# Gate and up projections of three feed-forwards as seven block products of 2x2 blocks

## Chip, cores and metric

The kernel runs on one core of a Trainium2 chip. The metric is device time in microseconds, the median over runs. Only the order and number of operations on the chip count; the host lays arrays out beforehand.

## Reference, cut to what matters

Two transformer blocks run one after the other on 512 tokens of width 1024, in float32. Between them they have five feed-forwards (numbered 0 to 4 here), all of inner width F = 2816. In a feed-forward every token row is normalised, projected twice (gate and up), combined and projected down:

```python
def swiglu_ffn(h, w_gate_up, w_down):
    g, u = jnp.split(h @ w_gate_up, 2, axis=-1)
    return (jax.nn.silu(g) * u) @ w_down

h = h + HALF_STEP * swiglu_ffn_2(rms_norm_2(h, ffn1_norm[layer]),
                               ffn1_w_gate[layer], ffn1_w_up[layer], ffn1_w_down[layer])
```

The second block has four of them: feed-forward 1 before a convolution module, 2 behind it, 3 before an attention layer, 4 behind it, the last before the final norm. Everything else (sparse attention, a recurrent mixer, cross attention, convolution, stick-breaking attention) stays as it is.

## The kernel before, in words

Activations lie transposed: x is eight tiles of 128 features by 512 tokens. The product of a weight tile and an activation tile in float32 is made of three matmuls in the shorter type float32r: every operand is split into a high part (ScalarE copies it, L127, or L133 with the norm's gain) and a low part (VectorE subtracts, L131, L134), and `mm3` (L170) adds high x high, high x low and low x high into one PSUM bank. `load_w` (L160) brings 128 output columns of a weight matrix (128 x 1024) in through SP's queue and splits them; there are three raw buffers and four of each split half.

`ffn` (L304) does a feed-forward in two halves of 11 F tiles. For each F tile it loads the gate and the up weights, makes both projections over all 512 tokens (8 K tiles x 3 matmuls each, L200), and `up` (L309) multiplies both with the tokens' inverse norms (row tile `rb`), applies Silu and splits the product into `hh` and `hl`. Then eight down products (L328, 11 F tiles x 3 matmuls) are added to x by the callback in `half_ffn` (L1031). With `head=2` (feed-forwards 0 and 1) the first two F tiles are made in token halves of 256, so that TensorE can start while the second half of the tokens is still being normalised (`post_norm_add`, L279, writes x on GpSimd at L294); with `tail=2` (0 and 4) the last two down products are made in halves.

The order on each engine's queue is set by a list scheduler of the framework, by program order and readiness in its own model of time; between `order_pe` and `free_pe` TensorE's order is the program's. `inv_rms_chain` (L233) places the few matmuls of the norm's sums between others, `tick` by `tick`. PSUM has eight banks under four names, which `mm_tile` and `at_tile` take in turn (`turn`, L65).

```python
for half in range(2):
    ...
    for p in range(FH):
        ...
            pg = mm_tile()
            proj(pg, g, xs)
            pu = at_tile()
            proj(pu, u, xs)
        h.append(up(p, pg, pu))
    ...
    for n in range(KT - nt):
        pd = mm_tile() if n % 2 else at_tile()
        down(half, n, load_down(n), pd, h)
        out_cb(half, n, pd, WHOLE)
```

Feed-forward 1 follows a norm that is finished token half by token half; 2 follows the convolution's output projection, whose callback (L1191) updates x tile by tile; 4 follows the attention's output projection in the same manner (L1351).

Of the kernel before, what the change touches and what calls it, by code (L numbers as in the profile page):

```python
# [25 lines left out]
NSA_H = 8  # L26
BUCKETS = 32
BW = 640
WHOLE = slice(0, S)
HALVES = (slice(0, S // 2), slice(S // 2, S))  # L30

# [17 lines left out]
def kernel(ctx: ExitStack, tc: tile.TileContext, t: dict, out: bass.AP):  # L49
# [24 lines left out]
    def mm_tile():  # L74
        return next_tile("mm")
# [91 lines left out]
        split(raw, hi, lo, pieces=pieces, hp=hp)  # L167
        return hi, lo

    def mm3(ps, lh, ll, rh, rl, start, stop):  # L170
        nc.tensor.matmul(ps, lh, rh, start=start, stop=False)  # L171
        nc.tensor.matmul(ps, lh, rl, start=False, stop=False)  # L172
        nc.tensor.matmul(ps, ll, rh, start=False, stop=stop)  # L173


    chain = []
# [127 lines left out]
    def ffn(fp, xs, st, wg, wu, wd, out_cb, head=0, tail=0, step=None):  # L304


        r = []

        def up(p, pg, pu):  # L309
            if not r:  # L310
                r.append(inv_rms(st)[1])
            rb = r[0]
            gr = fp.tile([P, S], F32, tag="gr", bufs=2, name=nm("gr"))
            nc.vector.tensor_tensor(gr, pg, rb, ALU.mult)
            nc.scalar.activation(gr, gr, AF.Silu)
            su = fp.tile([P, S], F32, tag="su", bufs=2, name=nm("su"))
            nc.vector.tensor_tensor(su, pu, rb, ALU.mult)  # L317
            nc.vector.tensor_tensor(su, su, gr, ALU.mult)
            hh = fp.tile([P, S], F32R, tag=f"hh{p}", name=nm("hh"))
            hl = fp.tile([P, S], F32R, tag=f"hl{p}", name=nm("hl"))  # L320
            split(su, hh, hl)
            return hh, hl

        def down(half, n, ws, pd, h, ts=WHOLE):
            for k in range(FH):
                hi, lo = ws[k // 6]
                sl = slice(k % 6 * P, (k % 6 + 1) * P)
                mm3(pd[:, ts], hi[:, sl], lo[:, sl], h[k][0][:, ts], h[k][1][:, ts], k == 0, k == FH - 1)  # L328
                tick()

        for half in range(2):
            h = []
            nh = 0 if half else head
            ws = [[load_w(w[n], D, pieces=4) for w in (wg, wu)] for n in range(nh)]
            pss = [(mm_tile(), mm_tile()) for n in range(nh)]
            for ts in HALVES:
                for n in range(nh):
                    projs(list(zip(pss[n], ws[n])), xs, ts)
            free_pe()
            if nh:  # L340
                order_pe()
                got = inv_rms_chain(st, 4, 6)
                pss.append(tuple(at_tile() for _ in range(2)))
                for ps, w in zip(pss[nh], (wg, wu)):
                    proj(ps, load_w(w[nh], D), xs)
                free_pe()
                r.append(got[1])
            for p in range(FH):
                n = half * FH + p
                if p < len(pss):  # L350
                    pg, pu = pss[p]
                else:
                    g = load_w(wg[n], D)
                    u = load_w(wu[n], D)
# [6 lines that stand above are left out]
            def load_down(n):  # L361
                return [load_w(wd[half, n][:, a * P : b * P], (b - a) * P) for a, b in ((0, 6), (6, FH))]

            nt = tail if half else 0
# [4 lines that stand above are left out]
            ws = {n: load_down(n) for n in range(KT - nt, KT)}  # L369
            pds = {n: mm_tile() if n % 2 else at_tile() for n in ws}  # L370
            if nt:
                order_pe()
            for ts in HALVES:
                for n in ws:
                    down(half, n, ws[n], pds[n], h, ts)
                    out_cb(half, n, pds[n], ts)
                if nt and step:
                    step(ts)

# [647 lines left out]
    def half_ffn(xs, st, idx, nxt, head=0, tail=0, step=None, ap=False):  # L1027
        st2, xs2 = {}, []

        def cb(half, n, ps, ts):  # L1030
            last_add[0] = nc.vector.scalar_tensor_tensor(x[n][:, ts], ps[:, ts], 0.5, x[n][:, ts], ALU.mult, ALU.add)  # L1031
            if half == 1:
                if nxt is not None:
                    xs2.append(split_x(n, nxt))
                square_acc(x[n], n, st2, ts, ap)

        with tc.tile_pool(name=f"fp{idx}", bufs=1) as fp:
            ffn(fp, xs, st, t[f"wg{idx}"], t[f"wu{idx}"], t[f"wd{idx}"], cb, head, tail,
                step and (lambda ts: step(st2, ts)))
        return xs2, st2  # L1040

    xs, st = half_ffn(xs, st, 1, "mix_norm_0", head=2)


    rt, rb = inv_rms(st)
    cs = ExitStack()
    cp = cs.enter_context(tc.tile_pool(name="cp", bufs=1))
# [466 lines left out]
```

## Time and profile before

| | |
|---|---|
| median of 3 runs | 2797.47 us (2797.16 to 2798.1) |
| the profiled execution's own time | 2799.96 us |
| its span, first to last instruction | 2798.2 us |
| mean granted TensorE clock | 0.994 of full speed |
| feed-forwards 1, 2 and 4 begin in the trace at about | 861, 1424 and 2425 us |

The profile is of one execution. PE is TensorE's matmuls, PEld its weight loads, DVE VectorE, ACT ScalarE, POOL GpSimd, SP the queue that issues most transfers. A matmul's start is recorded, its end is modelled, so rates are read from the distance of starts. A group of instructions shows how many there were, how long they were busy in all and on the mean, and how long the engine had been idle just before them and for whom.

### The profile page before, as it was taken

How to read it: one execution, taken by the hardware profiler on the slowest of the kernel's cores; microseconds unless marked ns; L12 is line 12 of the kernel's file. 1: busy time of each engine (PE TensorE's matmuls, PEld its weight loads, DVE VectorE, ACT ScalarE, POOL GpSimd, SP SyncE). 2: the span in 40 equal slices, each digit the busy share in tenths (PEclk: the TensorE clock that was granted, in tenths of full speed). 3: DMA queues.
4: the chain of work that ended last, by engine and by line, in shares of the span. 5: the costliest groups of instructions: out<-in, count | busy, mean ns of one | idle time of the engine just before them, and what ended most of it. 6: DMA issues, size and time to landing. Idle time of an engine off the chain costs nothing.

```text
span 2798.2 us, 35182 instructions
## 1 busy us (share of the span) xinstructions
PE 2731.0 (98%) x13750; PEld 2252.2 (80%) x13750; DVE 1465.1 (52%) x2270; ACT 1074.5 (38%) x1772; POOL 339.0 (12%) x451
## 2 busy tenths in 40 slices
PE   8999999999999999999899999999999997999998
PEld 6877988888888888885788888898888874788887
DVE  7666564643436434449754344534444489543443
ACT  5676544422334323331333233343223366332223
POOL 0133132200002000012210000100000136200001
PEclk9999999999999999999999999999999999999999
DMA  5312321223222233236332322323232320222322
GB/s 194 105 46 99 114 76 53 93 85 109 98 83 92 91 99 103 82 110 171 83 113 87 102 98 85 111 84 104 82 109 89 107 65 4 83 96 85 107 84 81
DMA packets 86923, 263.19 MB, mean 94 GB/s; under 512 B 9655, under 2 KB 13751, under 8 KB 86756
## 3 DMA queue, kind: packets, MB, share of 16 engines
q1 hardware_dynamic: 85148, 258.42, 29.6%
q10 hardware_dynamic: 1608, 2.52, 0.3%
q8 instruction: 108, 1.77, 0.3%
q14 instruction: 59, 0.48, 0.1%
HBM read 256.60 MB, written 4.30 MB: 93 GB/s over the span
## 4 chain that ended last, share of the span: by engine, by line
PE 79%; DVE 4%; issue 1%; DMA 1%; ACT 1%; POOL 0%; SPq 0%; DVEq 0%; ACTq 0%
PE sc L171 9%; PE sc L172 9%; PE sc L173 9%; PE mm L172 7%; PE mm L173 7%; PE mm L171 7%; PE tr L171 6%; PE tr L172 6%; PE tr L173 6%; PE po L171 3%; PE po L172 3%; PE po L173 3%; DVE wlo L131 1%; PE po L1311 1%; DVE c L1114 1%
## 5 line engine op out<-in xcount | busy, mean ns | idle before, releaser
L127 ACT ACTIVATE whi<-wraw 128x1024 fp32r<-128x1024 f32 (+3 forms) x518 | 492.3, 955 | 1287.4 <-PE sc L172 430.7
L131 DVE TENSOR_TENSOR wlo<-wraw,whi 128x1024 fp32r<-128x1024 f32 (+4 forms) x559 | 581.1, 1049 | 384.4 <-ACT whi L127 383.1
L171 PE MATMUL mm<-xh,whi 128*128 128x512 f32 (+1 forms) x760 | 287.7, 379 | 6.3 <-ACT whi L127 5.9
L172 PE MATMUL mm<-xl,whi 128*128 128x512 f32 (+1 forms) x760 | 286.9, 377 | 5.5 <-DVE xl L134 5.5
L173 PE MATMUL mm<-xh,wlo 128*128 128x512 f32 (+1 forms) x760 | 286.4, 377 | 0.0
L171 PE MATMUL sc<-xh,whi 128*128 128x512 f32 (+1 forms) x696 | 270.1, 388 | 0.0
L172 PE MATMUL sc<-xl,whi 128*128 128x512 f32 (+1 forms) x696 | 269.2, 387 | 0.0
L173 PE MATMUL sc<-xh,wlo 128*128 128x512 f32 (+1 forms) x696 | 269.2, 387 | 0.0
L172 PE MATMUL tr<-xl,whi 128*128 128x512 f32 (+1 forms) x592 | 222.8, 376 | 3.1 <-DVE xl L134 3.1
L171 PE MATMUL tr<-xh,whi 128*128 128x512 f32 (+1 forms) x592 | 223.1, 377 | 0.0
L173 PE MATMUL tr<-xh,wlo 128*128 128x512 f32 (+1 forms) x592 | 222.9, 376 | 0.0
L216 POOL TENSOR_TENSOR sqacc<-sq,sq 128x512 f32<-128x512 f32 (+1 forms) x11 | 16.3, 1486 | 1585.7 <-issue 896.0
L317 DVE TENSOR_TENSOR su<-sc,rb 128x512 f32<-128x512 f32 x80 | 55.3, 691 | 252.6 <-PE sc L173 252.6
L171 PEld LDWEIGHTS mm<-xh,whi 128*128 128x128 f32 x760 | 144.3, 190 | 33.2 <-ACT whi L127 5.9
L172 PEld LDWEIGHTS mm<-xl,whi 128*128 128x128 f32 x760 | 144.2, 190 | 31.9 <-DVE xl L134 7.1
L173 PEld LDWEIGHTS mm<-xh,wlo 128*128 128x128 f32 x760 | 144.2, 190 | 25.1 <-DVE wlo L131 0.3
L171 PEld LDWEIGHTS sc<-xh,whi 128*128 128x128 f32 x696 | 130.7, 188 | 29.6 <-issue 2.5
L173 PEld LDWEIGHTS sc<-xh,wlo 128*128 128x128 f32 x696 | 130.7, 188 | 26.5
L172 PEld LDWEIGHTS sc<-xl,whi 128*128 128x128 f32 x696 | 130.7, 188 | 26.3
L171 PE MATMUL sc<-hh,whi 128*128 128x512 f32 (+1 forms) x352 | 132.6, 377 | 0.0
L172 PE MATMUL sc<-hl,whi 128*128 128x512 f32 (+1 forms) x352 | 132.2, 376 | 0.0
L173 PE MATMUL sc<-hh,wlo 128*128 128x512 f32 (+1 forms) x352 | 132.2, 376 | 0.0
(531 smaller groups left out, 5554.0 us busy)
## 6 DMA issues: line engine op xcount, KB each, us to landing
wraw<-wg SPq DMA_DIRECT2D x110, 512.0 KB, 3.4
wraw<-wu SPq DMA_DIRECT2D x110, 512.0 KB, 3.4
wraw<-wd SPq DMA_DIRECT2D x80, 384.0 KB, 3.0
wraw<-wd SPq DMA_DIRECT2D x80, 320.0 KB, 2.8
wraw<-w_pw SPq DMA_DIRECT2D x24, 512.0 KB, 3.5
wraw<-w_in_f SPq DMA_DIRECT2D x15, 512.0 KB, 4.1
R<-glscr SPq DMA_DIRECT2D x28, 264.0 KB, 5.3
x<-xT SPq DMA_DIRECT2D x16, 256.0 KB, 5.9
```

Of the source, the lines that this page charges most:

```text
L127: last_hi[0] = nc.scalar.activation(hi[:, sl], src[:, sl], AF.Copy)
L131: nc.vector.tensor_tensor(lo[:, sl], src[:, sl], f32(hi[:, sl]), ALU.subtract)
L171: nc.tensor.matmul(ps, lh, rh, start=start, stop=False)
L172: nc.tensor.matmul(ps, lh, rl, start=False, stop=False)
L173: nc.tensor.matmul(ps, ll, rh, start=False, stop=stop)
L216: eng.tensor_tensor(state["acc"][:, ts], state["first"][:, ts], sq[:, ts], ALU.add)
L317: nc.vector.tensor_tensor(su, pu, rb, ALU.mult)
L1114: nc.vector.scalar_tensor_tensor(d, tap(k), v("w_dw", 31 * j + k), d, ALU.mult, ALU.add)
L1311: nc.tensor.matmul(po[64 * hx : 64 * hx + 64, j * P :], vsh[:, j, c0 : c0 + 64], PTs[hx][:, o : o + n_], start=j == 0, stop=j == NT - 1)
```

## The change

Feed-forwards 1, 2 and 4 get a new function, `ffn_blocks`. It takes two F tiles at a time and regards x (two K halves by two token halves) and the weights (two F tiles by two K halves) as 2x2 blocks. Seven products of sums and differences of blocks, instead of eight products of blocks, give the four blocks of the result (the scheme of Strassen in Winograd's form). Each product has gate and up side by side in one bank: 2 lanes x 4 K tiles x 3 matmuls of 256 tokens.

- `block_sums` forms four combinations of the token and K halves of x, once per feed-forward: 256-column operations on VectorE, a subtraction on GpSimd, and splits into high and low parts.
- `weights` loads the four weight blocks of a pair (gate and up side by side, 512 columns each), forms three further combinations with four 128 x 1024 additions on GpSimd, and splits seven operands instead of four.
- `product` accumulates into banks A (products 1, 4, 6, 7), B (2) and E (3, 5). What has to be kept between is copied out by ScalarE or subtracted by VectorE; `block` then does what `up` did, for 256 tokens at a time, with the up multiply on GpSimd for three of four blocks.
- The F tiles go in three chunks (8, 8 and 6 tiles) instead of two halves, each with its eight down products.
- `mm3` gets an argument that leaves out a check of accumulation groups; its three matmuls stay the same. After feed-forward 1 the turn of PSUM banks is set anew.
- The two-halves start of feed-forward 1 is replaced by the first two products of two pairs, which need the first token half alone.

The diff, cut to its core:

```diff
...
+BLOCKED = {1: "ffn1_norm_0", 2: "ffn2_norm_0", 4: "ffn2_norm_1"}
...
-    def mm3(ps, lh, ll, rh, rl, start, stop):
-        nc.tensor.matmul(ps, lh, rh, start=start, stop=False)
-        nc.tensor.matmul(ps, lh, rl, start=False, stop=False)
-        nc.tensor.matmul(ps, ll, rh, start=False, stop=stop)
+    def mm3(ps, lh, ll, rh, rl, start, stop, more=False):
+        for c, (a, b) in enumerate(((lh, rh), (lh, rl), (ll, rh))):
+            nc.tensor.matmul(ps, a, b, start=start and c == 0, stop=stop and c == 2, skip_group_check=more)
...
+    def ffn_blocks(fp, xs, st, gname, wg, wu, wd, out_cb, tail=0, step=None):
+        hs = []
+        a11 = [(h[:, LO], lo[:, LO]) for h, lo in xs[:4]]
+        a12 = [(h[:, LO], lo[:, LO]) for h, lo in xs[4:]]
+        a22 = [(h[:, HI], lo[:, HI]) for h, lo in xs[4:]]
+        sums = {}
+        raw = {}
+        for kp in range(2):
+            for i, q in enumerate((1, 2, 4, 3)):
+                raw[q, kp] = fp.tile([P, S], F32, tag=f"hh{4 * kp + i}", name=nm("sraw"))
+                sums[q, kp] = [fp.tile([P, S], F32R, name=nm(f"s{c}{q}{kp}")) for c in "hl"]
+        def block_sums(kp):
+            r1, r2, r3, r4 = (raw[q, kp] for q in (1, 2, 3, 4))
+            for kk in range(2):
+                k, c = 2 * kp + kk, slice(256 * kk, 256 * kk + 256)
+                g1, g2 = v(gname, k), v(gname, 4 + k)
+                nc.vector.tensor_scalar(r1[:, c], x[4 + k][:, HI], g2, None, ALU.mult)
+                nc.vector.scalar_tensor_tensor(r1[:, c], x[k][:, HI], g1, r1[:, c], ALU.mult, ALU.subtract)
+                nc.vector.scalar_tensor_tensor(r2[:, c], x[k][:, LO], g1, r1[:, c], ALU.mult, ALU.subtract)
+                nc.vector.scalar_tensor_tensor(r4[:, c], x[4 + k][:, LO], g2, r2[:, c], ALU.mult, ALU.subtract)
+                nc.gpsimd.tensor_tensor(r3[:, c], x[k][:, LO], x[k][:, HI], ALU.subtract)
+            split(r1, *sums[1, kp])
+            split(r2, *sums[2, kp], -1.0)
+            split(r4, *sums[4, kp])
+            for kk in range(2):
+                c = slice(256 * kk, 256 * kk + 256)
+                split(r3[:, c], *(t_[:, c] for t_ in sums[3, kp]), v(gname, 2 * kp + kk))
...
+        s1, s2, s3, s4 = (of_sum(q) for q in (1, 2, 3, 4))
+        def weights(m):
+            def load(q, pool, tag, bufs):
+                w = pool.tile([P, D], F32, tag=tag, bufs=bufs, name=nm("wb"))
+                cols = slice(q // 2 * 512, q // 2 * 512 + 512)
+                nc.sync.dma_start(w[:, :512], wg[2 * m + q % 2][:, cols])
+                nc.sync.dma_start(w[:, 512:], wu[2 * m + q % 2][:, cols])
+                return w
+            near, far = (fp, "wb", 5), (wp, "wraw", 3)
+            first = m == 0
+            b11 = load(0, *(far if first else near))
+            b21 = load(2, *(far if first else near))
+            b12 = load(1, *near)
+            b22 = load(3, *(near if first else far))
+            yield load_w(None, D, b11)
+            yield load_w(None, D, b21)
+            nc.gpsimd.tensor_tensor(b11, b11, b12, ALU.add)
+            yield load_w(None, D, b11)
+            nc.gpsimd.tensor_tensor(b11, b11, b22, ALU.add)
+            yield load_w(None, D, b11)
+            yield load_w(None, D, b22)
+            nc.gpsimd.tensor_tensor(b12, b22, b12, ALU.add)
+            yield load_w(None, D, b12)
+            nc.gpsimd.tensor_tensor(b21, b11, b21, ALU.add)
+            yield load_w(None, D, b21)
+        def product(ps, a, w, fresh):
+            hi, lo = w
+            for lane in range(2):
+                for k in range(4):
+                    sl = slice(lane * 512 + k * P, lane * 512 + k * P + P)
+                    mm3(ps[:, lane * 256 : lane * 256 + 256], hi[:, sl], lo[:, sl], a[k][0], a[k][1],
+                        fresh and lane == 0 and k == 0, lane == 1 and k == 3, not fresh)
+                    tick()
+        r = []
+        def block(ct, ts, p, ps=None):
+            g, u = ct[:, :256], ct[:, 256:]
+            gs, us = (g, u) if ps is None else (ps[:, :256], ps[:, 256:])
+            rb = r[0][:, ts]
+            nc.vector.tensor_tensor(g, gs, rb, ALU.mult)
+            nc.scalar.activation(g, g, AF.Silu)
+            (nc.gpsimd if ps is None else nc.vector).tensor_tensor(u, us, rb, ALU.mult)
+            nc.vector.tensor_tensor(u, u, g, ALU.mult)
+            split(u, hs[p][0][:, ts], hs[p][1][:, ts])
+        def pair(m, p):
+            ws = weights(m)
+            def ctile(q, bufs):
+                return fp.tile([P, S], F32, tag=f"c{q}", bufs=bufs, name=nm("c"))
+            A = ps_tile("mm")
+            product(A, a11, next(ws), True)
+            c1 = ctile(1, 2)
+            nc.scalar.activation(c1, A, AF.Copy)
+            yield
+            B = ps_tile("sc")
+            product(B, a12, next(ws), True)
+            def c11():
+                nc.vector.tensor_tensor(c1, c1, B, ALU.add)
+                block(c1, LO, p)
+            if r:
+                c11()
+            else:
+                pending.append(c11)
+            yield
+            E = ps_tile("tr")
+            product(E, s1, next(ws), True)
+            c3 = ctile(3, 2)
+            nc.scalar.activation(c3, E, AF.Copy)
+            yield
+            product(A, s2, next(ws), False)
+            c2 = ctile(2, 2)
+            nc.scalar.activation(c2, A, AF.Copy)
+            yield
+            product(E, s4, next(ws), False)
+            nc.vector.tensor_tensor(c2, E, c2, ALU.subtract)
+            block(c2, LO, p + 1)
+            yield
+            product(A, s3, next(ws), False)
+            nc.vector.tensor_tensor(c3, c3, A, ALU.subtract)
+            block(c3, HI, p + 1)
+            yield
+            product(A, a22, next(ws), False)
+            block(ctile(4, 1), HI, p, A)
+            yield
+        pending = []
...
+        for ci, (m0, m1) in enumerate(CHUNKS):
+            last = ci == len(CHUNKS) - 1
+            gens = {m: pair(m, 2 * (m - m0)) for m in range(m0, m1)}
+            if ci == 0:
+                for _ in range(2):
+                    next(gens[0])
+                free_pe()
+                order_pe()
+                got = inv_rms_chain(st, 6, 7)
+                for _ in range(2):
+                    next(gens[1])
+                free_pe()
+                r.append(got[1])
+                for kp in range(2):
+                    block_sums(kp)
+                for p in range(8):
+                    hs.append([fp.tile([P, S], F32R, tag=f"h{q}{p}", name=nm(f"h{q}{p}")) for q in "hl"])
+                for c11 in pending:
+                    c11()
+            for m in range(m0, m1):
+                steps = 5 if ci == 0 and m < 2 else 7
+                for i in range(steps):
+                    next(gens[m])
...
-            ffn(fp, xs, st, t[f"wg{idx}"], t[f"wu{idx}"], t[f"wd{idx}"], cb, head, tail,
-                step and (lambda ts: step(st2, ts)))
+            end = step and (lambda ts: step(st2, ts))
+            if idx in BLOCKED:
+                ffn_blocks(fp, xs, st, BLOCKED[idx], t[f"wg{idx}"], t[f"wu{idx}"], t[f"wd{idx}"], cb, tail, end)
+            else:
+                ffn(fp, xs, st, t[f"wg{idx}"], t[f"wu{idx}"], t[f"wd{idx}"], cb, head, tail, end)
...
+    turn.update(mm=["tr", "mm"], at=["sc", "po", "sc", "sc"])
```

The part left out at the end of `ffn_blocks` loads the down weights of a chunk as one tile of up to 1024 columns, makes the down products as before (`nk` F tiles x 3 matmuls of 512 tokens), and keeps the split tail of feed-forward 4.

## Rows read from the trace of the kernel before

**Rows 1.** Page, first part: busy us, share of span, instructions by engine.

```profile
PE 2731.0 (98%) x13750; PEld 2252.2 (80%) x13750; DVE 1465.1 (52%) x2270; ACT 1074.5 (38%) x1772; POOL 339.0 (12%) x451
```

**Rows 2.** Busy time of each engine by stretches, with clock and DMA.

```profile
core 0: us, PE busy (x) PEld busy (x) DVE busy (x) ACT busy (x) POOL busy (x), PEclk, DMA share, GB/s
867.50:874.30 6.80, 6.29 (x30) 5.86 (x29) 5.42 (x14) 1.52 (x3) 2.74 (x5) 0.50 0.39 136
846.00:1211.30 365.30, 361.26 (x1743) 305.85 (x1742) 172.99 (x241) 118.25 (x162) 23.26 (x25) 0.99 0.30 93
1405.00:1764.20 359.20, 359.20 (x1592) 297.53 (x1591) 160.60 (x195) 110.28 (x141) 16.08 (x10) 1.00 0.31 96
1604.70:1691.30 86.60, 86.60 (x384) 71.71 (x383) 39.10 (x46) 25.69 (x31) 0.00 (x0) 1.00 0.31 100
```

**Rows 3.** Timeline of PE, 512-column matmuls: start, us, line, operation, count.

```profile
1530.19 0.39 PE L172 MATMUL sc<-xl,whi 128*128 128x512 f32 x1
...
1535.18 0.39 PE L173 MATMUL tr<-xh,wlo 128*128 128x512 f32 x1
```

**Rows 4.** Timeline of PE, 256-column matmuls of feed-forward 1.

```profile
874.50 0.28 PE L173 MATMUL tr<-xh,wlo 128*128 128x256 f32 x1
...
878.33 0.28 PE L172 MATMUL mm<-xl,whi 128*128 128x256 f32 x1
```

**Rows 5.** Groups by line and shape: busy us, mean ns, idle before.

```profile
L131 DVE TENSOR_TENSOR wlo<-wraw,whi 128x1024 fp32r<-128x1024 f32 x317 | 390.2, 1233 | 197.9 <-ACT whi L127 197.0 <-PE tr L1295 0.3
L318 DVE TENSOR_TENSOR su<-su,gr 128x512 f32<-128x512 f32 x110 | 75.8, 691 | 8.4
L293 DVE TENSOR_TENSOR yf<-yf,sc 128x256 f32<-128x256 f32 x16 | 6.1, 413 | 1.3 <-PE sc L270 1.3
L127 ACT ACTIVATE whi<-wraw 128x1024 fp32r<-128x1024 f32 x332 | 350.7, 1060 | 854.7 <-PE sc L172 264.7 <-PE mm L172 191.3 <-PE tr L172 181.1
L127 ACT ACTIVATE hh<-su 128x512 fp32r<-128x512 f32 x110 | 69.4, 633 | 86.9 <-DVE su L318 86.9
L1376 POOL TENSOR_TENSOR x<-x,rs 128x256 f32<-128x256 f32 x4 | 2.8, 732 | 2.7 <-ACT rs L1372 2.7
```

**Rows 6.** Timeline of POOL, an addition with VectorE idle.

```profile
2756.71 1.29 POOL L218 TENSOR_TENSOR sqacc<-sqacc,sq 128x512 f32<-128x512 f32 x1 [6.20 <-ACT sq L211]
```

**Rows 7.** Timelines of POOL and DVE in the convolution.

```profile
1283.07 1.73 POOL L1118 TENSOR_TENSOR macc<-conv,conv 128x512 f32<-128x512 f32 x1 [1.83 <-DVE conv L1116]
1284.76 1.75 POOL L216 TENSOR_TENSOR sqacc<-sq,sq 128x512 f32<-128x512 f32 x1
...
1282.91 0.74 DVE L1114 SCALAR_TENSOR_TENSOR c<-gl,vec,c 128x512 f32<-128x512 f32 x1
1283.57 1.78 DVE L1114 SCALAR_TENSOR_TENSOR conv<-gl,vec,conv 128x512 f32<-128x512 f32 x1
1285.27 1.78 DVE L1114 SCALAR_TENSOR_TENSOR c<-gl,vec,c 128x512 f32<-128x512 f32 x1
1286.97 0.74 DVE L1114 SCALAR_TENSOR_TENSOR conv<-gl,vec,conv 128x512 f32<-128x512 f32 x1
```

**Rows 8.** Timelines of PE and POOL at the start of feed-forward 1.

```profile
863.36 0.39 PE L172 MATMUL mm<-xl,whi 128*128 128x256 f32 x1 [1.57 <-DVE xl L134]
...
866.29 0.39 PE L172 MATMUL mm<-xl,whi 128*128 128x256 f32 x1 [1.95 <-DVE xl L134]
...
874.28 7.11 POOL L294 TENSOR_TENSOR x<-x,yf 128x256 f32<-128x256 f32 x8 [1.28 <-DVE yf L293]
```

**Rows 9.** Timeline of DVE at the start of feed-forward 2.

```profile
1426.30 0.74 DVE L1192 SCALAR_TENSOR_TENSOR x<-mm,vec,x 128x512 f32<-128x512 f32 x1
1426.96 0.73 DVE L134 SCALAR_TENSOR_TENSOR xl<-x,vec,xh 128x512 fp32r<-128x512 f32 x1
```

More of the change, by code (lines that the diff above doesn't have):

```diff
@@ L376, in ffn, with of_sum, down, load_down @@
                     out_cb(half, n, pds[n], ts)
+                if nt and step:
+                    step(ts)
+    LO, HI = HALVES
+    CHUNKS = ((0, 4), (4, 8), (8, FT // 2))
+    def ffn_blocks(fp, xs, st, gname, wg, wu, wd, out_cb, tail=0, step=None):
[25 more added lines that the diff above has]
+                split(r3[:, c], *(t_[:, c] for t_ in sums[3, kp]), v(gname, 2 * kp + kk))
+        def of_sum(q):
+            return [tuple(t_[:, 256 * (k % 2) : 256 * (k % 2) + 256] for t_ in sums[q, k // 2]) for k in range(4)]
+        s1, s2, s3, s4 = (of_sum(q) for q in (1, 2, 3, 4))
[81 more added lines that the diff above has]
+        pending = []
+        def down(n, w, pd, nk, ts=WHOLE):
+            hi, lo = w
+            for k in range(nk):
+                sl = slice(k * P, k * P + P)
+                mm3(pd[:, ts], hi[:, sl], lo[:, sl], hs[k][0][:, ts], hs[k][1][:, ts], k == 0, k == nk - 1)
+                tick()
+        for ci, (m0, m1) in enumerate(CHUNKS):
[21 more added lines that the diff above has]
+                    next(gens[m])
+            nk = 2 * (m1 - m0)
+            def load_down(n):
+                w = wp.tile([P, D], F32, tag="wraw", bufs=3, name=nm("wb"))
+                for half in range(2):
+                    a, b = max(2 * m0, half * FH), min(2 * m1, half * FH + FH)
+                    if a < b:
+                        nc.sync.dma_start(w[:, (a - 2 * m0) * P : (b - 2 * m0) * P],
+                                          wd[half, n][:, (a - half * FH) * P : (b - half * FH) * P])
+                return load_w(None, nk * P, w[:, : nk * P])
+            nt = tail if last else 0
+            for n in range(KT - nt):
+                pd = mm_tile() if n % 2 else at_tile()
+                down(n, load_down(n), pd, nk)
+                out_cb(last, n, pd, WHOLE)
+            ws = {n: load_down(n) for n in range(KT - nt, KT)}
+            pds = {n: mm_tile() if n % 2 else at_tile() for n in ws}
+            if nt:
+                order_pe()
+            for ts in HALVES:
+                for n in ws:
+                    down(n, ws[n], pds[n], nk, ts)
+                    out_cb(last, n, pds[n], ts)
```

## Prediction

> **What bounds the kernel now.** I began with the busy shares: TensorE is busy 98% of the span, VectorE 52%, ScalarE 38%, GpSimd 12% [rows 1]. A busy TensorE is not yet a full one, so the table by stretches came next: in the two feed-forwards shown whole, and in a stretch inside the gate and up products, TensorE is busy 99 to 100% of the time, at a granted clock of 0.99 to 1.00, which is the 2.4 GHz level [rows 2]. Then the timeline of TensorE, since the ends of matmuls are modelled but their starts are not. Between 1530.19 and 1535.18 there are 22 starts of 512-column matmuls, 0.2268 us apart [rows 3]; between 874.50 and 878.33 there are 32 starts of 256-column ones, 0.1197 us apart, each with a weight load of its own [rows 4]. So these stages are a gapless stream of matmuls, and time is number of matmuls by spacing. A half-width matmul costs 53% of a whole one: about 13 ns of each don't scale with columns.
>
> **The TensorE term.** A pair of F tiles now takes 2 tiles x 2 matrices x 8 K tiles x 3 parts = 96 matmuls of 512 columns: 96 x 0.2268 = 21.77 us. After, it takes seven products of 2 lanes x 4 K tiles x 3 = 24 matmuls of 256 columns: 168 x 0.1197 = 20.11 us. That is 1.66 us less; 11 pairs in three feed-forwards give 54.9 us. Feed-forward 1 already runs its first two tiles in token halves, 192 x 0.1197 = 22.98 us, which adds 1.2. Term: **-56 us**. An eighth of the work goes, but the 13 ns return more than a third of it. The Trainium skill (TensorE: Matmul & The Clock Gate, Back-to-back issue gap) gives a gap of columns over 2.4 GHz plus 2.5 ns; by it a pair would go from 20.7 to 18.3 us, and the term would be -80 us. Rows 3 and 4 measure these very instructions, so their spacing is used.
>
> **Down products, loads, ScalarE.** The down products stay 22 x 8 x 3 = 528 whole matmuls per feed-forward. Three chunks instead of two halves add eight updates of x, 0.69 us each at the price of a like 512-column operation [rows 5], on VectorE beside down products of 24 x 0.2268 = 5.4 us: nothing, and at most 8 x 0.69 x 3 = 17 us if nothing covered them. Weights come as twice as many transfers of half the size, the same bytes, with the DMA engines 0.30 to 0.31 busy [rows 2]; SP has no other work there: nothing. ScalarE gets per pair seven weight copies at 1.06 us, three copies and eight half-width operations, the latter at no more than the whole-width 0.63 [rows 5]: 7.4 + 1.9 + 5.0 = 14.3 of 20.1 us at most, covered. The changed rotation of PSUM banks adds no instruction; the cover is the other banks, the price otherwise one drain of 0.69 us [rows 5] a tile. The row-norm sums move to the second pair, and only the blocks' first multiply waits for them.
>
> **The start of each blocked feed-forward.** Product three needs sums over both token halves and all eight x tiles. Ahead of it stand the first two products of two pairs, 96 x 0.1197 = 11.5 us. For one half of K VectorE does eight 256-column operations, three 512-column splits and two 256-column ones: 10 x 0.41 + 3 x 0.69 = 6.2 us [rows 5], so 12.4 us for both; the first half can begin before the last x tile. In feed-forward 1 that arithmetic also needs the second token half, which GpSimd updates from 874.28 to 881.39 [rows 8]. TensorE began the first token half just before 863.36 and already waited twice for its splits, 1.57 and 1.95 us [rows 8]; the same 11.5 us of work, so started, end about 877. The sums cannot be ready before 881.4 plus the last quarter of the sums and a split, some 4 us: a wait of about 9 us, bounds 4 and 15. There the clock also fell to half for 6.8 us [rows 2]; such a stretch costs up to 3.4, which is in the upper bound. In feed-forward 2 the last x tile is written at 1427.04 [rows 9] while TensorE still has 11.5 us to do: about 3 us, bounds 0 and 6. Feed-forward 4 starts after the same kind of projection: 3 more. Term: **+15 us**, 4 to 27.
>
> **VectorE and GpSimd.** In the stretch inside the gate and up products GpSimd has no instruction now [rows 2]. After, each pair asks of it four 1024-column adds and three 256-column multiplies. A 256-column one takes 0.732 us [rows 5], a 512-column one alone 1.29 [rows 6]; by that slope 1024 columns take 2.41 us, an estimate. Sum: 4 x 2.41 + 3 x 0.73 = 11.8 us. VectorE gets seven weight subtractions at 1.233 and eleven 256-column operations at 0.413 that read two SBUF tiles: 13.2 us; and 3 x 0.69 + 2 x 0.41 = 2.9 us that read a PSUM bank [rows 5].
>
> Each fits in 20.1 us. Together they don't run freely: where GpSimd adds and VectorE combines two SBUF tiles, a VectorE operation of 0.74 us becomes 1.78, a GpSimd one of 1.29 becomes 1.75, and the two alternate with a period of 1.69 us against 0.74 + 1.29 = 2.03 [rows 6, 7]. VectorE's operations with a PSUM input stay at 0.413 amid GpSimd's adds [rows 5, 8]. So they take turns and give 0.33 us back at each turn. Per pair: 13.2 + 11.8 - 7 x 0.33 = 22.7; the other eleven VectorE operations overlap their neighbours by 0.08 [rows 7], giving 21.8. With none of the 2.9 us under a GpSimd turn it is about 24.5. I take 23.1, the middle, three above TensorE's 20.1.
>
> That excess need not reach TensorE. In the down products VectorE has 1.23 + 0.69 = 1.9 us of work in each 5.4, and four weight buffers let it run three products ahead: three subtractions and two adds, about 8 us per chunk. The last pair's block arithmetic, some 5 us, runs on into the down products. A chunk of four pairs has 4 x 3.0 = 12 us of excess against 13 of cover, one of three has 9. Only the first chunk has no down products ahead of it: 12 - 5 = 7 us show, in three feed-forwards **+21 us**; bounds 0 and 33 x 4.4 = 145.
>
> **Sum.** -56 + 15 + 21 = -20 us. The profiled execution took 2799.96 us, span 2798.2 with 1.8 around it; the median shown is 2797.47, 2.5 lower. So 2780 for such an execution, **2777 us** for the median.
>
> **Rivals.**
> *The turns set the pace.* If weight preparation cannot run ahead, because the add that makes the next weights waits for the subtraction that reads the last, TensorE idles in every pair. VectorE's queue is in order: behind a subtraction waiting for GpSimd stand the block operations that free PSUM, and TensorE waits for those. The price is 33 x 1.7 = 56 us to 145 us in place of 21: 2812 to 2901, at the middle 33 x 3.0 = 99, 2855. It decides from 20.11 + (56 - 15) / 33 = 21.4 us a pair. For it: 21.8 is already above that. Against it: the cover counted above. Chance 0.33.
> *Turns without overlap.* If operations excluded each other for their whole length, a pair would take 25.0 us and up, and the time would be 2797 - 41 + 33 x 4.9 = 2918. The period of 1.69 against 2.03 [rows 7] speaks against it: 0.02. The Trainium skill (SBUF — State Buffer, Who interferes with whom) says of such pairs of operations that the loser fully blocks; the rows agree that it waits, but show a sixth of the length overlapped.
> *The bank wait.* The sixth product is subtracted out of its bank before the seventh may accumulate there. That is 0.69 us plus what stands ahead on VectorE, up to a 1.23 subtraction and a GpSimd turn of 2.4. The next pair's first product, 24 x 0.1197 = 2.9 us, can fill it if it is issued between. If 1.2 us a pair stays, 33 x 1.2 = 40 replaces the 21: 2797, no change. Chance 0.15.
>
> **How the numbers follow.** The forecast case holds 0.50; its own range is 2755 to 2792. A measurement of this kernel tells 0.2%, 5.6 us, from no change. The bank wait at smaller and larger sizes puts 0.03 into faster and spreads to the sides: faster 0.53, same 0.12, slower 0.35. The range runs from 2752, where nearly nothing shows but the starts, to 2838, the lower half of the first rival.
>
> **What would show it.** Right: in the interior of a chunk 256-column starts 0.12 us apart, TensorE's idle time gathered at the starts of the blocked feed-forwards and in their first chunks, GpSimd over half busy there. Wrong: waits of TensorE for weight halves all through the chunks, or for VectorE's subtractions out of the same bank; VectorE's 1024-column subtractions well over 1.5 us on the mean mean the turns decide. A spacing other than 0.12 would break the first term, a half clock outside the starts the rest.

## The result, and the profile after

The changed kernel takes 2901.18 us (median of 4 runs, 2900.15 to 2902.72), the kernel before 2797.78 beside it (2797.16 to 2798.78): ratio 1.037, interval 1.0352 to 1.0388. It is 103 us slower, where 20 us faster was forecast, and it lies above the range. The profiled execution took 2902.72 us, with a span of 2900.9.

First the page's first part and its chain of waits, both of the changed kernel:

```profile
PE 2723.5 (94%) x16000; PEld 2339.8 (81%) x16000; DVE 1942.8 (67%) x2699; ACT 1241.4 (43%) x2108; POOL 823.2 (28%) x694
...
PE 56%; DVE 20%; issue 7%; ACT 2%; DMA 1%; POOL 1%; SPq 0%; DVEq 0%; ACTq 0%; POOLq 0%
```

Beside [rows 1] TensorE has 2250 matmuls more and is busy 7.5 us less, since they are half as wide; but its share fell from 98% to 94%. VectorE gained 478 us of busy time and GpSimd 484, and a fifth of the chain now runs over VectorE.

Where the time went is read from landmarks in TensorE's timeline: the last matmul of the down products of feed-forwards 0, 1, 2 and 3. The table has the stretches between them, in us, for the profiled executions (spans) of the two kernels and of four experiments that are told below.

| | run-in | feed-forward 1 | convolution, ff 2 | ff 3 | attention, ff 4, end | span |
|---|---|---|---|---|---|---|
| before | 861.4 | 370.4 | 552.9 | 451.5 | 562.0 | 2798.2 |
| after | 860.2 | 416.2 | 579.9 | 451.5 | 593.2 | 2900.9 |
| additions left out | 863.2 | 370.2 | 536.1 | 451.5 | 556.3 | 2777.3 |
| GpSimd's work on VectorE | 864.1 | 379.5 | 545.5 | 451.5 | 561.5 | 2802.0 |
| plain first tiles | 859.4 | 388.7 | 563.8 | 451.5 | 577.0 | 2840.4 |
| both of the last two | 861.8 | 366.2 | 536.2 | 451.5 | 545.3 | 2761.0 |

Nothing is lost outside the three blocked feed-forwards: +45.8, +27.0 and +31.2 us. Inside a chunk a pair takes 24.5 us, read from one copy out of the bank of product three (L503) to that of the next pair; the sum of the prediction had 20.1 for TensorE and 23.1 for the turns, and before it was 21.8. Four stretches show what lies behind this: one pair in the interior, a stretch of down products, and two at the start of feed-forward 1.

```profile
core 0: us, PE busy (x) PEld busy (x) DVE busy (x) ACT busy (x) POOL busy (x), PEclk, DMA share, GB/s
1083.94:1108.49 24.55, 21.18 (x171) 20.36 (x169) 24.03 (x24) 11.24 (x18) 15.01 (x8) 1.00 0.26 86
1138.00:1157.00 19.00, 19.00 (x86) 15.74 (x85) 10.04 (x13) 6.03 (x7) 0.00 (x0) 1.00 0.35 111
872.66:890.30 17.64, 0.34 (x4) 0.14 (x2) 17.54 (x27) 10.20 (x21) 14.22 (x13) 0.64 0.43 149
890.00:905.00 15.00, 6.36 (x25) 5.56 (x26) 15.00 (x19) 6.16 (x10) 6.94 (x3) 0.61 0.00 0
```

In the pair VectorE is full (24.03 of 24.55) and TensorE is not. In the down products GpSimd does nothing and VectorE is busy half the time. At the start TensorE stands nearly still for 17.6 us, and the granted clock falls to 0.64 and 0.61 on the mean of the two stretches, between its levels of 1.2 and 2.4 GHz; in a gapless stream it was 1.00 [rows 2]. The groups of VectorE and GpSimd in that same pair (count, then busy us and mean ns, then idle time before):

```profile
L133 DVE TENSOR_TENSOR wlo<-wb,whi 128x1024 fp32r<-128x1024 f32 x7 | 9.0, 1297 | 0.0
L473 DVE TENSOR_TENSOR c<-c 128x256 f32<-128x256 f32 x5 | 8.7, 1730 | 0.0
L133 DVE TENSOR_TENSOR hl<-c,hh 128x256 fp32r<-128x256 f32 x4 | 4.4, 1106 | 0.5 <-ACT hh L129 0.5
L470 DVE TENSOR_TENSOR c<-c,rb 128x256 f32<-128x256 f32 x3 | 3.3, 1091 | 0.0
...
L449 POOL TENSOR_TENSOR wb<-wb,wb 128x1024 f32<-128x1024 f32 x2 | 6.7, 3362 | 0.0
L472 POOL TENSOR_TENSOR c<-c,rb 128x256 f32<-128x256 f32 x3 | 4.2, 1405 | 6.1 <-DVE c L492 5.1 <-DVE c L514 1.0
```

VectorE's long subtractions keep their length (1.30 against 1.233 in [rows 5]); the short operations, 0.41 us when free, take 1.1 to 1.7 on the mean. The timelines of the two engines show why; their columns are start, length, engine and line, and VectorE's rows stand first:

```profile
1085.75 1.21 DVE L133 TENSOR_TENSOR wlo<-wb,whi 128x1024 fp32r<-128x1024 f32 x1
1086.89 0.95 DVE L470 TENSOR_TENSOR c<-c,rb 128x256 f32<-128x256 f32 x1
1087.76 2.62 DVE L133 TENSOR_TENSOR hl<-c,hh 128x256 fp32r<-128x256 f32 x1
1090.30 2.62 DVE L473 TENSOR_TENSOR c<-c 128x256 f32<-128x256 f32 x1
...
1087.52 2.58 POOL L446 TENSOR_TENSOR wb<-wb,wb 128x1024 f32<-128x1024 f32 x1
1090.17 2.46 POOL L451 TENSOR_TENSOR wb<-wb,wb 128x1024 f32<-128x1024 f32 x1
```

The two short VectorE operations of 2.62 us are recorded as long as the additions of GpSimd that they came up against: one addition, one operation of VectorE, and so on. That the recorded length holds the wait is shown by the first experiment below, where the same operations are back at 0.41. By [rows 5] VectorE's own work in the pair is 7 x 1.23 + 11 x 0.41 + 2.9 (its operations with a PSUM input) = 16.0 us (the stretch holds five operations of L473, the first and the last cut by its ends; a pair has four); it is busy for 24.0, so 8.0 us are waits.

### The profile page after: what moved, and what is told of

Same layout as the page of the kernel before. It is cut to its first block, busy times and chain, and to the rows that moved or that the text cites. A ratio compares the mean times of both kernels' runs of the same rounds, so it can differ in the third digit from the quotient of the medians.

```text
span 2900.9 us, 41122 instructions
## 1 busy us (share of the span) xinstructions
PE 2723.5 (94%) x16000; PEld 2339.8 (81%) x16000; DVE 1942.8 (67%) x2699; ACT 1241.4 (43%) x2108; POOL 823.2 (28%) x694
## 4 chain that ended last, share of the span: by engine, by line
PE 56%; DVE 20%; issue 7%; ACT 2%; DMA 1%; POOL 1%; SPq 0%; DVEq 0%; ACTq 0%; POOLq 0%
PE mm L175 17%; PE sc L175 17%; PE tr L175 14%; PE po L175 5%; DVE c L473 5%; DVE wlo L133 4%; DVE hl L133 1%; DVE c L470 1%; DVE c L1318 1%; DVE xl L136 1%; DVE conv L1318 1%; DVE rm L1485 1%; ACT whi L129 1%; DVE c L510 1%; DVE c L514 0%
## 5 line engine op out<-in xcount | busy, mean ns | idle before, releaser
L129 ACT ACTIVATE whi<-wraw 128x1024 fp32r<-128x1024 f32 (+3 forms) x290 | 276.1, 960 | 595.0 <-PE sc L175 189.7
L133 DVE TENSOR_TENSOR wlo<-wraw,whi 128x1024 fp32r<-128x1024 f32 (+4 forms) x319 | 334.5, 1061 | 223.7 <-ACT whi L129 223.3
L129 ACT ACTIVATE whi<-wb 128x1024 fp32r<-128x1024 f32 (+1 forms) x303 | 310.7, 1035 | 291.0 <-PE mm L175 93.7
L133 DVE TENSOR_TENSOR wlo<-wb,whi 128x1024 fp32r<-128x1024 f32 (+1 forms) x303 | 396.9, 1317 | 39.8 <-ACT whi L129 39.5
L175 PE MATMUL mm<-xh,whi 128*128 128x256 f32 (+1 forms) x1000 | 334.4, 334 | 56.8 <-DVE c L514 29.8
L175 PE MATMUL mm<-xl,whi 128*128 128x256 f32 (+1 forms) x1000 | 331.0, 331 | 10.6 <-DVE xl L136 10.6
L175 PE MATMUL mm<-xh,wlo 128*128 128x256 f32 (+1 forms) x1000 | 330.5, 331 | 3.1 <-DVE wlo L133 3.1
L175 PE MATMUL mm<-sh,wlo 128*128 128x256 f32 (+1 forms) x544 | 158.5, 291 | 17.6 <-DVE wlo L133 17.5
L175 PE MATMUL tr<-sh,whi 128*128 128x256 f32 (+1 forms) x544 | 159.8, 294 | 15.4 <-ACT c L503 10.8
L175 PE MATMUL mm<-sh,whi 128*128 128x256 f32 (+1 forms) x544 | 158.3, 291 | 10.7 <-ACT whi L129 9.9
```

What stands on the lines that cost most here:

```text
L129: last_hi[0] = nc.scalar.activation(hi[:, sl], src[:, sl], AF.Copy)
L133: nc.vector.tensor_tensor(lo[:, sl], src[:, sl], f32(hi[:, sl]), ALU.subtract)
L175: nc.tensor.matmul(ps, a, b, start=start and c == 0, stop=stop and c == 2, skip_group_check=more)
```

## The experiments

A time without a ratio is of one run. The runs of the kernel before that were taken beside these spread from 2795.4 to 2807.0 us, so 10 us of time say little by themselves; a pair in the second and third chunks repeats within 0.2 us.

**The additions, left out and moved.** Three kernels first: without the four additions of `weights`, so that three combinations are not formed; with a bank of its own for product seven, which leaves out of its block what bank A holds already; with all that GpSimd had been given put on VectorE.

```diff
-            nc.gpsimd.tensor_tensor(b11, b11, b12, ALU.add)
```

(and the three like it; the first experiment)

> Leaves out the four 1024-column weight additions of each pair (three weight combinations are not formed); everything else stays. Theory T (turns): VectorE is the bound inside the blocked feed-forwards because each of its operations with two SBUF inputs waits out GpSimd's additions; without them the period of a pair falls from 24.55 us to 20.1 to 20.9, and the time from 2901 to about 2780, 20 either way. Rival B (bank): the period is set by TensorE waiting for the subtraction out of the bank that the seventh product accumulates in; the additions only run beside it: period at least 22.5, time 2845 or more. Rival L (load): VectorE has too many operations of its own: period unchanged within 0.5 us.

2779.16 us, and 20.2 us a pair in every chunk, behind the first two pairs of a feed-forward. TensorE doesn't wait at all in the stretch from 1040 to 1060 us, here in the table by stretches of this run:

```profile
1040.00:1060.00 20.00, 20.00 (x169) 20.00 (x168) 16.60 (x23) 11.38 (x18) 2.56 (x3) 1.00 0.30 105
```

VectorE is busy 16.60 us there with its 23 operations of a pair, and the short ones are free of waits (L469 is L473 of the changed kernel):

```profile
L133 DVE TENSOR_TENSOR hl<-c,hh 128x256 fp32r<-128x256 f32 x4 | 1.7, 415 | 0.0
L469 DVE TENSOR_TENSOR c<-c 128x256 f32<-128x256 f32 x4 | 1.7, 414 | 0.0
```

So the TensorE term is as forecast (20.2 measured, 20.11 worked out), and the additions, together with what waits for them, cost 2900.9 - 2777.3 = 123.6 us of span.

```diff
-            product(A, a22, next(ws), False)
-            block(ctile(4, 1), HI, p, A)
+            G7 = ps_tile("po")
+            product(G7, a22, next(ws), True)
+            block(ctile(4, 1), HI, p, G7)
```

> The seventh product starts a bank of its own, so it doesn't wait for the subtraction of the sixth; it leaves out the products that were to stand in that bank already. T: VectorE stays full and the wait moves to another product; period 24.2 to 24.6 us, time 2890 to 2903. B: the 1.95 us wait a pair goes, 33 x 1.8 = 59 us, time about 2842. L: as T.

2933.13 us and 24.1 to 25.8 us a pair in the second and third chunks: slower still. In the changed kernel TensorE's longest wait in a pair was for the subtraction out of product six's bank (L514). The longest of its waits from 1060 to 1120 us, first in the changed kernel, then in this one:

```profile
PE mm L175 <- DVE c L514: 3.8, 3, 1.7
PE mm L175 <- DVE wlo L133: 1.6, 2, 0.8
PE mm L175 <- ACT whi L129: 1.3, 3, 0.4
```

```profile
PE mm L175 <- ACT whi L129: 4.5, 2, 2.3
PE mm L175 <- DVE wlo L133: 1.4, 2, 0.8
```

The wait on the bank is gone and a wait for weight halves of about the same size has taken its place. The bank wait was where VectorE's lateness showed, not its cause. This kernel is 32 us slower than the changed one, and 20 of them lie in the second and third chunks. There the trace shows a lower granted clock, here in one pair:

```profile
1078.97:1104.21 25.24, 22.24 (x168) 21.77 (x168) 23.23 (x24) 11.54 (x19) 14.12 (x8) 0.91 0.26 86
```

Every pair of these chunks that takes 25.0 us or more has a clock of 0.90 or 0.91, where the changed kernel had 1.00 in all; TensorE had waited up to 2.3 us for a weight half. The pairs at 0.96 to 0.99 take 24.1 us, 0.3 less than their like in the changed kernel. Read from these, the bank itself is worth some 0.3 us a pair, and what makes this kernel slower there goes with the clock; its first chunks were not looked into.

The third puts the additions, the up multiply of `block` and the subtraction for r3 on VectorE (`nc.gpsimd` becomes `nc.vector` in six places).

> The four weight additions, the up multiply of three blocks and the subtraction in the sums move from GpSimd to VectorE; nothing is left out. T: VectorE's own work is then about 19.7 us a pair by durations without GpSimd beside it, period 20.1 to 21.0, time 2765 to 2800. L: VectorE was busy 24.0 of 24.55 us already, 5.6 us more make about 29.6 a pair and the time about 3070. B: the subtraction stands behind more work on VectorE, period 25 or more, time 2915 or more.

2799.82 us beside 2800.41, ratio 0.9995 (0.9984 to 1.0005), 20.2 us a pair. From 1026.50 to 1101.00, 3.7 pairs, the table of this run reads

```profile
1026.50:1101.00 74.50, 74.50 (x623) 74.50 (x622) 67.80 (x100) 41.80 (x64) 0.00 (x0) 1.00 0.32 108
```

VectorE does more work and is less busy: 91% against 98%. Of the 123.6 us 98.9 come back by changing engines alone. The weights come by the same transfers as before, so it is not a wait for them that stretched the pair.

Then which of GpSimd's operations it is. One kernel moves only the up multiply, another only the additions.

> Only the up multiply of three blocks moves from GpSimd to VectorE; the weight additions stay. T: VectorE gains 3 x 0.34 us of work a pair and is spared three turns of 0.59: period 23.5 to 24.0, time about 2901 - 33 x 0.8 = 2875. Rival L (VectorE has too much work of its own): period 25.5, time 2930.

2878.69 us, 23.5 us a pair.

> The changed kernel with the four weight additions of a pair on VectorE; the up multiply and the sums' subtraction stay on GpSimd. Turns theory: it is the additions, four of GpSimd's long operations, that hold VectorE up, and three 256-column multiplies a pair are too short to matter once those are gone; a pair takes 20.1 to 20.6 us inside a chunk and the time is 2790 to 2815 us, near the 2800 of the kernel with all three on VectorE. Rival: the multiplies cost on their own what they cost beside the additions, where moving them took 1.0 us off a pair (24.5 to 23.5); then a pair takes some 21.2 us and the time is about 2830 us.

2794.48 us, 20.2 us a pair: the additions are the cost, and the multiplies cost nothing without them. The groups from 1030 to 1090 us show that they now wait in their turn:

```profile
L133 DVE TENSOR_TENSOR wlo<-wb,whi 128x1024 fp32r<-128x1024 f32 x20 | 25.3, 1271 | 2.0 <-ACT whi L129 2.0
...
L472 POOL TENSOR_TENSOR c<-c,rb 128x256 f32<-128x256 f32 x9 | 23.1, 2561 | 42.7 <-DVE c L492 20.4 <-DVE c L510 14.6 <-DVE c L514 7.6
```

A multiply of GpSimd takes 2.56 us instead of 0.73 [rows 5]; nobody on the path waits for it.

**More of the same.** If turns set the pace, more GpSimd work must lengthen the pair. The first try added two 512-column additions on a spare tile to each pair, which depend on nothing in it:

> Two further 512-column additions on GpSimd in each pair, on a spare tile that nobody else reads: 2.6 us of GpSimd, which is busy 15.0 of 24.55 us. T: VectorE waits for them, 2 x 1.15 us a pair: period 26.3 to 26.9, time about 2901 + 33 x 2.0 = 2967. B and L: GpSimd has room for them: period within 0.3 us of 24.55, time within 10 us of 2901.

2944.16 us, but 24.5 us a pair as before. GpSimd's groups from 881 to 980 us hold 22 of these additions (feed-forward 1 has 11 pairs): the scheduler had run all of them in the first chunk, so the run says nothing of the interior:

```profile
L486 POOL TENSOR_TENSOR spare<-spare 128x512 f32<-128x512 f32 x22 | 32.7, 1487 | 0.5
```

The next two tie the extra work to the pair, behind its last addition: two additions that read b11 and b21, or five memsets into b11, which read nothing.

```diff
             nc.gpsimd.tensor_tensor(b21, b11, b21, ALU.add)
+            for _ in range(2):
+                nc.gpsimd.tensor_tensor(spare, b11[:, :512], b21[:, :512], ALU.add)
```

> The changed kernel with two further 512-column additions on GpSimd in each pair, which read the pair's own sums and so cannot run ahead (those of the earlier run all ran in the first chunks, where its 43 us went). T: VectorE waits for them: period 24.55 + 2 x 1.15 = 26.9 us, at least 26.0; time 2901 + 33 x 2.0 = 2965. Rivals (GpSimd's own queue or its chain of additions sets the period, or TensorE's order): GpSimd was busy 15.0 of 24.55 us, so 2.6 more fit: period within 0.5.

2939.68 us, mostly 25.3 to 25.5 us a pair: +0.9, where 2.3 were expected. The direction holds, the size doesn't. One such pair, at full clock:

```profile
1648.36:1673.68 25.32, 22.67 (x184) 22.03 (x183) 22.69 (x20) 11.13 (x18) 16.59 (x9) 1.00 0.19 64
```

> The same place and about the same GpSimd time (5 x 0.52 us) spent on writing constants into a tile that is no longer needed, which reads nothing from SBUF. T in the form that only reads of two SBUF tiles are in each other's way: period within 0.5 us of 24.55, time 2890 to 2915. If any GpSimd work holds VectorE up, or the longer hold of that buffer: 26.5 or more, as in the run with additions.

2911.33 us; a pair took 24.4 to 24.6 us in most places and 24.9 to 25.5 in others. Two of its pairs:

```profile
1078.67:1103.29 24.62, 21.18 (x170) 20.36 (x168) 24.10 (x24) 11.23 (x20) 17.21 (x13) 1.00 0.27 87
1103.29:1128.41 25.12, 22.42 (x170) 21.82 (x168) 24.60 (x24) 11.23 (x20) 17.17 (x13) 0.93 0.26 84
```

In the second and third chunks every longer pair has a granted clock of 0.93, and every pair at 1.00 takes what it took in the changed kernel. So at full clock five memsets of 0.525 us cost next to nothing, and two additions (2 x 1.35 us, as much GpSimd time) cost 0.9 us a pair; by whole times it is 10 us against 38. GpSimd's groups from 1070 to 1120 us, of the additions and of the memsets:

```profile
L455 POOL TENSOR_TENSOR spare<-wb,wb 128x512 f32<-128x512 f32 x4 | 5.4, 1350 | 0.3
```

```profile
L453 POOL MEMSET wb<- 128x512 f32 x10 | 5.2, 525 | 6.6 <-DVE wlo L133 6.2
```

So it is neither GpSimd's time as such nor what it writes that holds VectorE up; that leaves its reads of SBUF.

**The start.** The first tiles as before the change, four F tiles in feed-forward 1 and two in the others (their weights come into `load_w`'s own raw buffers again), cut short:

```diff
-            gens = {m: pair(m, 2 * (m - m0)) for m in range(m0, m1)}
+            gens = {m: pair(m, 2 * (m - m0)) for m in range(m0, m1) if 2 * m >= np_}
...
+                    pss = [(mm_tile(), mm_tile()) for n in range(2)]
+                    for ts in HALVES:
+                        for n in range(2):
+                            projs(list(zip(pss[n], w2[n])), xs, ts)
```

Once with GpSimd's work kept, once with all of it on VectorE as well:

> The changed kernel with its first tiles as before the change (four F tiles of feed-forward 1, two of feed-forwards 2 and 4), all of GpSimd's additions kept. The landmarks of the changed kernel put some 40 us into the start of feed-forward 1 and some 13 into each of the other two, besides the turns; 10 us stay at feed-forward 1, and four pairs fewer at 24.5 us instead of 21.8 give 11 more: 2835 us, 2820 to 2860, and a pair inside a chunk stays at 24.5 us. If the start cost no more than the 15 us of the prediction and the rest came from the turns, the time would be 2901 - 15 - 11 = 2875 us.

2842.22 us, 24.4 to 24.6 us a pair.

> As the run with all arithmetic on VectorE, but each blocked feed-forward begins with F tiles made as before the change (four in feed-forward 1, two of them in token halves; two in 2 and 4), and the seven products begin behind them; nothing is left out. Theory S: what kept that run at the time of before is the start alone, where product three waits for sums over all of x; with 21.8 us or more of other products ahead the sums are ready in time: 10 + 10 + 9 pairs at 1.66 us give 48 us, less some 10 for what remains and 4 that the attention stage lost: 0.980 to 0.990 of before, about 2765 to 2775. Rival: the loss at the start is that of the first weights (seven splits and four sums per pair on VectorE, 98% full), and only moves: ratio 0.995 to 1.002.

2761.99 us (2760.31 to 2762.91), ratio 0.987 (0.9854 to 0.9886), 20.2 us a pair. This version beats both kernels. What it leaves in feed-forward 1 is two waits of TensorE before its first block product, here from 862 to 980 us:

```profile
PE sc L259 <- DVE sqacc L220: 5.7, 1, 5.7
PE mm L175 <- DVE xl L136: 3.5, 2, 2.0
```

Two last kernels start from it: one without the line `turn.update(...)`, one without it and with six plain tiles in feed-forward 1 (`np_ = 6`).

> The kernel with plain first tiles and everything on VectorE (2762.0 us, ratio 0.987), without the line that sets the turn of PSUM banks anew after feed-forward 1. In every kernel with that line the stretch from the end of feed-forward 3 to the start of feed-forward 4 took 3.8 to 4.3 us longer than before the change, with TensorE's waits there for bank names in another order. If the line is the cause, those 4 us come back there: 2756 to 2760 us, ratio 0.985 to 0.9865, unless the old turn costs as much elsewhere. If the line has no part in it, 2762 us again, within 2.

2765.52 us, ratio 0.988 (0.9865 to 0.9894). The stretch after feed-forward 3, up to the matmuls of the next norm's sums, doesn't shorten (202.2 us against 202.7), and the premise was wrong: the 4 us were read from where one sort of matmul ends and the next begins. In the kernel with plain tiles 18 matmuls of feed-forward 4 stand ahead of that mark that came behind it before, 18 x 0.2268 = 4.1 us. Feed-forward 4's first matmul itself starts 187.5 us after the last of feed-forward 3 in this run, 187.9 with the line, 188.3 before the change. In the changed kernel, where the mark was another, some 22 matmuls of the attention's output projection had moved ahead of it, with TensorE busy all along; its row in the table by stretches:

```profile
2450.00:2474.00 24.00, 23.94 (x110) 17.37 (x109) 5.90 (x11) 5.63 (x9) 2.83 (x3) 1.00 0.00 1
```

Nothing had been lost there.

> As the run before, with six plain F tiles in feed-forward 1 instead of four. After the fourth tile TensorE stood still for 9.2 us there (5.7 for the sums of squares, 3.5 for a low part of x), 15 us from one stream to the next against 5.6 before the change. If that idle time is lack of work whose operands are there, two more plain tiles fill up to 9 us of it and cost 1.7: 2748 to 2756 us. If it is the chain of the norm itself, which everything behind waits for, nothing is filled and the time is 2 us above the run before.

2762.62 us, ratio 0.9868 (0.9852 to 0.9885), and feed-forward 1 took 366.7 us against 365.5 in the run before: +1.2, so nothing is filled. The wait for the sums of squares is 6.6 us now; it is the norm's chain that everything behind waits for. That the whole is 3 us faster than the run before comes from between feed-forwards 1 and 2, where the stretch is 7.3 us shorter, with a run-in 3.2 us longer; why was not looked into.

## Why the prediction was wrong

The run without additions splits the difference into the prediction's terms. By spans and landmarks: TensorE 33 x (20.2 - 21.77) - 1.2 = -53; starts, what is left of that run's stretches beyond it, +30; additions and their turns +124; run-in +2 in that run. Sum +103, as measured; the forecast was -56 + 15 + 21.

**The TensorE term** held: 20.2 us a pair wherever TensorE isn't held up, against 20.11. By the Trainium skill's gap, which the page gives for an isolated matmul (TensorE: Matmul & The Clock Gate, Back-to-back issue gap), a pair would be 18.3 us, an estimate; the measured 20.2 speaks for the spacing of [rows 4].

**"I take 23.1, the middle"** failed: a pair takes 24.5, the upper bound. Its working let VectorE's PSUM operations, 2.9 us a pair, run half under a turn of GpSimd. By the rows VectorE's 16.0 us and GpSimd's 4 x 2.4 + 3 x 0.73 = 11.8 add up to 27.8, and only 3.3 are given back, about the 0.33 us at each turn and the small overlaps that [rows 7] had shown, and nothing for PSUM. The additions themselves were priced right (2.39 to 2.41 us alone). The Trainium skill (SBUF — State Buffer, Who interferes with whom) says that a VectorE operation with two SBUF inputs contends with a GpSimd operation that reads SBUF, not with one that only writes it. The two extra additions (+0.9 us a pair) and the memsets (under 0.1 at full clock) agree. The full block that the page states comes near in effect: 25.0 us a pair by whole lengths, 24.5 measured.

**"That excess need not reach TensorE"** failed worse. From the end of one chunk's down products to the end of the last chunk's, the changed kernel takes 1276.4 - 1039.5 = 236.9 us in feed-forward 1, the one without additions 217.4. Seven pairs of 4.3 us excess are 30.1; 19.5 show, so a chunk covers 5.3 us, not 13. The difference is the same 19.5 in feed-forwards 2 and 4, so of the 124 us some 58 lie in the second and third chunks. The first chunks, which have no cover ahead and where the additions meet the sums, lost 26.5, 24.2 and 17.3 us by the same landmarks, where 7 each was forecast.

The run ahead itself came as the prediction had it: three additions ended before the down products did, at 1175.7, all in their last 14 us. It spares TensorE little more than one pair's excess; from the second pair of a chunk on a pair takes 24.4 to 24.6 us again. Why three products ahead save so little is not shown. More room was there: in the 19 us from 1138 on GpSimd has no instruction and VectorE 9 us free. But GpSimd sat idle for 29.74 us, until 1161.94, nearly all of it in these down products, for a subtraction by VectorE that frees the raw weights. That subtraction waits for ScalarE's copy, and the copies of the next pair's weights come one behind each down product, after a wait for its last matmul. GpSimd's timeline, then ScalarE's:

```profile
1161.94 2.39 POOL L444 TENSOR_TENSOR wb<-wb,wb 128x1024 f32<-128x1024 f32 x1 [29.74 <-DVE wlo L133]
1164.41 2.41 POOL L449 TENSOR_TENSOR wb<-wb,wb 128x1024 f32<-128x1024 f32 x1
1172.88 2.39 POOL L446 TENSOR_TENSOR wb<-wb,wb 128x1024 f32<-128x1024 f32 x1 [6.06 <-DVE wlo L133]
```

```profile
1159.54 1.06 ACT L129 ACTIVATE whi<-wb 128x1024 fp32r<-128x1024 f32 x1 [4.33 <-PE po L175]
1164.98 1.06 ACT L129 ACTIVATE whi<-wb 128x1024 fp32r<-128x1024 f32 x1 [4.38 <-PE mm L175]
```

By these waits it is the four split buffers, which the down weights pass through too, that hold the work back until then; a kernel with more of them was not run.

**The start, +15**, was mis-sized: +30 without the additions, by feed-forward 18, 1 and 12 against 9, 3 and 3. Plain first tiles bring 60.5 us back in the changed kernel, of which four pairs at 21.8 instead of 24.5 are 11. In feed-forward 1 the order assumed failed: of the "first two products of two pairs" only those of one pair ran before TensorE stood still. TensorE's longest waits from 860 to 990 us begin with

```profile
PE mm L175 <- ACT whi L129: 18.2, 3, 17.3
```

It waits for the copy of the second pair's first weights, and these were loaded late. Most of the blocks' raw buffers (`wb`) lie in the pool that is opened when the one with feed-forward 0's y (`yf`) is closed, and SP's queue holds their transfers until GpSimd has added the last of y to x. SP's wait for GpSimd between 845 and 880 us, and GpSimd's additions to x:

```profile
SPq L431 <- POOL x L296: 13.7, 1, 13.7
```

```profile
871.24 7.03 POOL L296 TENSOR_TENSOR x<-x,yf 128x256 f32<-128x256 f32 x8 [2.93 <-DVE yf L295]
```

SP's next transfer, the one that brings the up half of the weights in question, and the same by size and us to its landing:

```profile
878.30 0.33 SPq L431 DMA_DIRECT2D wb<-wg  x1
...
880.78 0.41 SPq L432 DMA_DIRECT2D wb<-wu  x1
```

```profile
wb<-wu SPq DMA_DIRECT2D x1, 256.0 KB, 5.6
```

ScalarE's copy:

```profile
888.61 0.63 ACT L129 ACTIVATE sh<-sraw 128x512 fp32r<-128x512 f32 x1 [2.19 <-DVE sraw L410]
889.14 1.04 ACT L129 ACTIVATE whi<-wb 128x1024 fp32r<-128x1024 f32 x1
```

The weights are there at 880.78 + 5.6 = 886.4, of a wait that ends at 890.2. Only the last 2.7 us to the copy go to ScalarE's queue, where it stands behind splits of the sums that wait for VectorE, which is busy 17.54 of 17.64 us there. In the run without additions the copy waits for the transfer itself:

```profile
889.52 1.06 ACT L129 ACTIVATE whi<-wb 128x1024 fp32r<-128x1024 f32 x1 [0.94 <-DMA wb<-wu]
```

So the step that failed here is the loads, put at nothing because SP has no other work: when their buffers come free was not asked. No run placed these buffers elsewhere and kept the block order; the plain first tiles change both. The fallen clock (0.64, 0.61) comes on top. In feed-forward 4 it is part of the 12 us too: in the run without additions TensorE idles for 6.0 us of the first 23.5, and the mean granted clock of 0.72 costs up to 0.28 x 23.5 = 6.6, an estimate, where the prediction had counted a lower clock in feed-forward 1 alone:

```profile
2409.50:2433.00 23.50, 17.51 (x97) 16.02 (x95) 21.23 (x35) 12.16 (x19) 5.31 (x6) 0.72 0.40 135
```

**What else was costed at nothing** was right as far as it shows: TensorE's stream in the down products has no gap (19.00 of 19.00), and the turn of PSUM banks lost nothing in the attention.

**The rivals.** "The turns set the pace" is what happened: 24.5 us a pair against the 21.4 from which it was to decide, and 2901 is its upper end, though part of that is the starts. Its case against, the cover, was the step that failed. The bank wait was seen, as a symptom, worth some 0.3 us a pair of the 1.2 that its case counted. One sign was named wrongly: the subtractions of 1024 columns did not grow past 1.5 us; the short operations did.

## What to carry to other kernels

An addition of two SBUF tiles on GpSimd is not spare work where VectorE combines SBUF tiles too: the addition takes 2.4 us of GpSimd and nearly 2 from VectorE ((24.03 - 16.60) / 4), which would do it in 1.22, so count the two engines' lengths as one sum and put it on the faster. Idle time is cover only from the moment at which the buffers let the work begin; look for the row that says when. The same holds for the loads of a new first stage: ask what must end before their buffers are free.

## What the runs showed of the hardware

A GpSimd addition held a 0.41 us VectorE operation for 2.6 us, and when VectorE carried the additions a 0.73 us GpSimd multiply took 2.56: either engine is the one that is held. Five memsets on GpSimd (0.525 us each) lengthened no pair whose granted clock was 1.00 (24.4 to 24.6 us with and without them). In the kernel with both parts changed VectorE's 1024-column additions took 1.22 us, as long as a subtraction.
